# Row maxima of an attention encoder from the queries' high halves, four key blocks of a query tile in one go

## The chip, the cores and the metric

The kernel runs on one core of one Trainium2 chip. The metric is the device time of one execution in microseconds, as the median of several runs; smaller is better. PE is the matrix engine, DVE the vector engine, ACT the scalar engine, POOL the general-purpose engine, SP the engine that issues most DMAs. PSUM is the memory into which PE writes; DVE and ACT read it.

## The reference

Two layers, each on 2048 positions of 1024 features. A layer normalises, projects to seven column groups, mixes one half by a gated spatial product within chunks of 128 positions, and runs attention on the other half: 8 query heads, 2 key/value heads of 64 channels, query and key normalised and rotated, every query against all 2048 keys.

```python
sc = jnp.einsum('bqkgd,bskd->bkgqs', qblk, k).astype(jnp.float32) * scale
p = jax.nn.softmax(sc, axis=-1).astype(v.dtype)
return jnp.einsum('bkgqs,bskd->bqkgd', p, v)
```

The concatenated halves, each multiplied by a gate, go through an output projection, a second normalisation and the residual sum. Softmax gives the same result whatever number is subtracted from a whole row of scores, as long as nothing overflows; the kernel subtracts an approximate row maximum.

## The kernel before

All float32 operands of the large products are split into two float16 halves, high and low, and each product is made of three float16 products. Queries lie in DRAM as `q_d[group][head]`, two halves of 64 channels each by 512 positions; keys lie in SBUF as `k_st`, where the key's high half stands twice, in rows 0 to 63 and again in rows 64 to 127, and as `k_lo`, its low half with two rows of ones.

A layer has two stages. In the first the projections run, 24 matmuls to an accumulation (`pp`), and a list of background jobs with due times (`bg`) is stepped along with them; each step gives out up to two jobs that are due. In the second stage attention runs over units: a unit is one of 4 groups of 512 queries (`qb`) with one of 8 heads, 32 units a layer. A unit goes over 16 key blocks of 128 keys; an iteration `k` of the main loop is one key block, 512 in a layer. In an iteration PE makes the scores (`sp`, keys by 512 queries, two matmuls: `k_st` with both query halves stacked in 128 rows, and `k_lo` with the query's high half and the maxima in 66 rows). ACT takes the exponential twice, to float16 (`p_parts`) and to float32 (`p_f`); POOL, and DVE in 15 of 100 iterations, subtract the one from the other for the low half; three iterations later PE multiplies both halves with the values (`po`, 12 matmuls). Jobs for certain iterations stand in a table `later` (written by `at`), and a list `fill` is spread over the iterations; it holds the output projection of the group before (`pout`). It begins 16 iterations after a group's last unit.

The shift of the scores must be known before a unit's attention begins. So the row maxima are made ahead, with queries in the output's rows: for each of a unit's 4 query tiles of 128 queries (`j`) and each of 4 key blocks of 512 keys (`c`), PE makes one matmul `pmax` of the tile's queries, high and low half stacked in 128 rows, against `k_st`, and DVE reduces it to a column of `mx` (`max_step`; 16 steps to a unit, 1024 in all). `max_row` takes the maximum over the 4 columns, `stack_max` transposes it (`t<-ident,m_neg`) and stores it as two float16 rows. The first 8 units of a layer are done as background jobs at the end of the projection stage (the calls in `before`, L860 on DVE), one step per job. The other 24 are placed in the attention iterations, 16 steps of a unit spread over 20 iterations, so that four iterations in five have one.

Every PSUM tile, `sp`, `pmax`, `pp`, `pout`, `po`, `py` and the transposes alike, comes from one pool of 8 buffers, each a whole bank. A buffer given out again waits for the last reader of what it held. PE, DVE, ACT and POOL work off their instructions strictly in the written order; in the attention stage all of it is pinned (the class `Pinned`, whose helper is line 87, so most instructions there carry L87).

Of the kernel before, what the change touches and what calls it, by code (L numbers as in the profile page):

```python
# [14 lines left out]
ALU = mybir.AluOpType  # L15
AX = mybir.AxisListType
# [3 lines left out]
P = 128  # L20
D = 1024
ND = D // P
GRP = 512
TPG = GRP // P
NH = 8
HD = 64
# [16 lines left out]
def encoder(ctx: ExitStack, tc, x, w_in, w_out, pre_g, post_g, ln_a_g, ln_a_b,  # L43
            spatial_w, spatial_b, q_norm_g, k_norm_g, rope, out):
    nc = tc.nc
# [3 lines left out]
    NG = S // GRP  # L49
# [18 lines left out]
    def f_t(name, n=GRP, dt=F32):  # L68
        return fp.tile([P, n], dt, name=name, tag="f")
# [4 lines left out]
    def ps_t(name):  # L74
        return psum.tile([P, GRP], F32, name=name, tag="ps", bufs=8)
# [14 lines left out]
    PE, ACT, DVE, POOL = Pinned(nc.tensor), Pinned(nc.scalar), Pinned(nc.vector), Pinned(nc.gpsimd)  # L90
# [9 lines left out]
    q_d = [dram.tile([NH, 2, HD, GRP], F16, name=f"q_d{g}") for g in range(NG)]  # L100
# [86 lines left out]
    bg = Background()  # L187
# [616 lines left out]
    def attend(l, kv, nxt):  # L804

        k_st, k_lo, _, v16 = kv
# [25 lines left out]
        def at(k, f):  # L832
            later.setdefault(k, []).append(f)

        state = [Obj() for _ in units]
        pairs = [Obj() for _ in range(len(units) // 2)]

        def load_qm(u):
            qb, h = units[u]
            s = state[u]  # L840
            s.qm = f_t("q_m", dt=F16)
            nc.sync.dma_start(s.qm, q_d[qb][h].rearrange("a d t -> (a d) t"))
            s.mx = small.tile([P, TPG, NG], F32, name="mx", bufs=3)

        def load_q(u):
            qb, h = units[u]
            s = state[u]
            s.qs = f_t("q_st", dt=F16)
            nc.sync.dma_start(s.qs, q_d[qb][h].rearrange("a d t -> (a d) t"))
            s.q2 = f_t("q2", dt=F16)  # L850
            nc.sync.dma_start(s.q2[0:HD], q_d[qb][h, 0])
            nc.sync.dma_start(s.q2[HD:HD + 2], m_d[qb][h])

        def max_step(u, n, pe, dve):
            s = state[u]
            j, c = n // NG, n % NG
            kv = units[u][1] // (NH // NKV)
            ps = ps_t("pmax")
            pe.matmul(ps, s.qm[:, j * P:(j + 1) * P], k_st[:, kv, c * GRP:(c + 1) * GRP], start=True, stop=True)
            dve.tensor_reduce(s.mx[:, j, c:c + 1], ps, AX.X, ALU.max)  # L860

        def max_row(u, dve):
            s = state[u]
            s.m = small.tile([P, TPG], F32, name="m_neg", bufs=3)
            dve.tensor_reduce(s.m, s.mx, AX.X, ALU.max, negate=True)

        def stack_max(u, pe, act, dve):
            s = state[u]
            qb, h = units[u]
            ps = ps_t("t2")  # L870
            pe.transpose(ps[0:TPG, 0:P], s.m, ident)
            for i in range(2):
                rows = small.tile([TPG, P], F16, name="m_rows", bufs=4)
                if i == 0:
                    hi = rows
                    act.activation(rows, ps[0:TPG, 0:P], AF.Copy, bias=EXP_SHIFT)
                else:
                    dve.scalar_tensor_tensor(rows, ps[0:TPG, 0:P], EXP_SHIFT, hi, ALU.add, ALU.subtract)
                nc.sync.dma_start(m_d[qb][h, i].rearrange("(t p) -> t p", p=P), rows)
# [327 lines left out]
        steps = TPG * NG  # L1207
        span = ((len(units) - 1) * NT - 16) // (len(units) - pre)

        def before():  # L1210

            n0 = 0
            for u in range(pre):
                bg.add(max(n0 - 10, 0), lambda u=u: load_qm(u))
                for n in range(steps):
                    bg.add(n0 + 4 + n, lambda u=u, n=n: max_step(u, n, PE, nc.vector))
                bg.add(n0 + steps + 6, lambda u=u: max_row(u, nc.vector))
                bg.add(n0 + steps + 8, lambda u=u: stack_max(u, PE, nc.scalar, nc.vector))
                n0 += steps
            bg.add(n0 + 4, lambda: load_q(0))  # L1220
            bg.add(n0 + 4, lambda: load_qm(pre))

        def first_wo():
# [4 lines left out]
            for f in wout_steps(range(4), nc.scalar, nc.vector):  # L1228
                f()

        yield before, first_wo
        both = [w_t([P, 8, GRP], "p_parts", F16) for _ in range(2)]
        both = [b[:, n] for b in both for n in range(8)]
# [18 lines left out]
        for u in range(pre, len(units)):  # L1252
            k0 = (u - pre) * span
            if k0 >= 8:
                at(k0 - 8, lambda u=u: load_qm(u))
            for n in range(steps):
                at(k0 + n * span // steps, lambda u=u, n=n: max_step(u, n, PE, DVE))
            at(k0 + span + 1, lambda u=u: max_row(u, DVE))
            at(k0 + span + 5, lambda u=u: stack_max(u, PE, ACT, DVE))

# [51 lines left out]
        for k in range(end + 4):  # L1312
            if k < total:
                u, i = k // NT, k % NT
                s = state[u]
                kv = units[u][1] // (NH // NKV)
# [23 lines left out]
            if 0 <= kb < total:  # L1340
                u, i = kb // NT, kb % NT
                s = state[u]
                kv = units[u][1] // (NH // NKV)
# [16 lines left out]
        n = 0  # L1360
# [27 lines left out]
    for l in range(DEPTH):  # L1388
        k_t = big_t([P, 2, NKV, S], "k_t", F16)
        kv = [k_t[:, 0], k_t[:, 1]]  # L1390
        v_t = big_t([P, 2, NT * NKV * HD], "v_st")
        kv.append(v_t.bitcast(F32)[:, 0].rearrange("p (t k d) -> p t k d", t=NT, k=NKV))
        v_h = v_t.bitcast(F16).rearrange("p a n -> p (a n)")[:, 4 * NT * NKV * HD - NT * NKV * VW:]
        kv.append(v_h.rearrange("p (t k d) -> p t k d", t=NT, k=NKV))
        att = attend(l, kv, layers[l + 1] if l + 1 < DEPTH else None)
        layers[l].run(kv, layers[l].first, *next(att))
        for _ in att:
            pass
# [40 lines left out]
```

## Time and profile before

| what | us |
|---|---|
| median of three runs | 2554.7 |
| lowest and highest run | 2548.59, 2555.02 |
| the profiled execution's own time | 2549.72 |
| its span from first to last instruction | 2547.9 |
| PE busy in it | 2461.1 |
| DVE, ACT, POOL busy | 1833.9, 1558.3, 1151.0 |
| attention stage of layer 1, about | 593 to 1259 |
| attention stage of layer 2, about | 1854 to 2512 |

In a row of the page's groups stand the source line, engine, operation, what is written and read, the tile's size, the count, the busy time and the mean duration of one in ns, then the idle time before them and who ended it. PE's durations are modelled and overlap, so the spacing of starts is what a matmul costs. ACT's and DVE's records overlap a little too. In a row of the timeline stand the start in us, the time from the start of the first to the end of the last instruction merged in it, and the count; in brackets, the idle time before it and who ended it.

### The profile page before, as it was taken

The numbers are of one execution on the slowest core, as the hardware profiler recorded it, in microseconds if no ns is written. First come the engines' busy times: TensorE is split into PE (matmuls) and PEld (weight loads), VectorE is DVE, ScalarE is ACT, GpSimd is POOL, SyncE is SP. The second block draws the span as 40 slices with busy tenths as digits, with TensorE's granted clock in tenths as the row PEclk, the third lists the DMA queues.
The fourth block names the chain that finished last, engine by engine and source line by source line (L and its number), as shares of the span: only waits on it lengthen the run. The fifth ranks groups of instructions, "written<-read, shape, count | busy, mean of one in ns | idle before, by whom it ended". The sixth has DMA issues, their size and how long they took to land. (4 is left out here: it accounts for less than half of the span.)

```text
span 2547.9 us, 61817 instructions
## 1 busy us (share of the span) xinstructions
PE 2461.1 (97%) x24938; PEld 1634.4 (64%) x24938; DVE 1833.9 (72%) x4138; ACT 1558.3 (61%) x3219; POOL 1151.0 (45%) x968
## 2 busy tenths in 40 slices
PE   6999999999999999999989999999999999999997
PEld 5888876445665666665569887754456666656653
DVE  6676677886767787778377666778777767776765
ACT  6643212116998888898645522111289988888884
POOL 0000110005888777787530011100078877777875
PEclk9999999999999999999989999999999999999999
DMA  5254212211221221221433622122222212221213
GB/s 189 88 170 126 59 37 87 67 55 60 78 72 57 74 78 52 84 88 60 158 125 100 194 76 67 50 80 56 67 68 66 74 53 74 62 67 52 70 53 129
DMA packets 224963, 211.64 MB, mean 83 GB/s; under 512 B 44834, under 2 KB 194978, under 8 KB 224676
## 3 DMA queue, kind: packets, MB, share of 16 engines
q1 hardware_dynamic: 224676, 207.69, 26.5%
q8 instruction: 195, 3.19, 0.5%
q14 instruction: 92, 0.75, 0.1%
HBM read 140.92 MB, written 66.72 MB: 81 GB/s over the span
## 5 line engine op out<-in xcount | busy, mean ns | idle before, releaser
L87 POOL TENSOR_TENSOR p_parts<-p_f,p_parts 128x512 f16<-128x512 f32 x872 | 1040.3, 1208 | 568.1 <-ACT p_f L87 514.6
L87 ACT ACTIVATE p_parts<-sp 128x512 f16<-128x512 f32 x1024 | 629.8, 615 | 160.3 <-PE sp L87 125.9
L87 PEld LDWEIGHTS <-p_parts 128*128 128x128 f16 x12288 | 511.7, 97 | 257.5 <-DVE p_parts L87 7.4
L87 PE MATMUL pp<-w_hl,hT 128*128 128x256 f16 x5376 | 637.8, 275 | 8.3 <-ACT w_hl L324 4.7
L87 ACT ACTIVATE p_f<-sp 128x512 f32<-128x512 f32 x1024 | 629.9, 615 | 0.0
L87 DVE TENSOR_REDUCE mx<-pmax 128x1 f32<-128x512 f32 x768 | 512.9, 680 | 120.8 <-PE pmax L87 119.1
L87 PEld LDWEIGHTS <-hT 128*128 128x128 f16 x5376 | 520.6, 99 | 83.7 <-issue 13.0
L87 PE MATMUL po<-v_st,p_parts 128*128 128x65 f16 (+1 forms) x12288 | 545.6, 193 | 11.5 <-DVE p_parts L87 6.4
L87 PE MATMUL pout<-wo,y_t 128*128 128x512 f16 x1488 | 462.7, 379 | 0.2
L87 PE MATMUL pmax<-k_t,q_m 128*128 128x512 f16 x1024 | 389.2, 381 | 8.7 <-DVE mx L860 7.7
L87 PE MATMUL sp<-q,k_t 66*128 66x512 f16 x1024 | 390.8, 382 | 0.0
L87 PE MATMUL sp<-q_st,k_t 128*128 128x512 f16 x1024 | 388.4, 379 | 1.9 <-DVE mx L87 0.9
L87 PE MATMUL pp<-hT,w_hl 128*128 128x512 f16 x1536 | 380.7, 383 | 0.0
L87 PEld LDWEIGHTS <-w_hl 128*128 128x128 f16 x1536 | 148.3, 99 | 181.7 <-issue 15.0
L87 PEld LDWEIGHTS <-y_t 128*128 128x128 f16 x1488 | 144.8, 98 | 170.0 <-issue 3.5
L860 DVE TENSOR_REDUCE mx<-pmax 128x1 f32<-128x512 f32 x256 | 169.2, 681 | 28.9 <-PE pmax L87 28.4
L87 PEld LDWEIGHTS <-q_m 128*128 128x128 f16 x1024 | 101.1, 99 | 119.7 <-issue 1.4
L427 POOL TENSOR_TENSOR fa<-fa,gain_q 128x512 f32<-128x512 f32 x16 | 21.6, 1352 | 325.1 <-DMA fa<-in_rope_dram 175.0
L524 POOL TENSOR_TENSOR fl<-fv,fh 128x512 fp32r<-128x512 f32 x32 | 42.6, 1351 | 251.3 <-ACT fh L523 224.7
L87 DVE TENSOR_TENSOR p_parts<-p_f,p_parts 128x512 f16<-128x512 f32 x152 | 119.6, 787 | 38.8 <-ACT p_f L87 38.4
L555 ACT ACTIVATE pp<-fa 128x512 f32<-128x512 f32 x32 | 19.3, 602 | 188.8 <-DVE fa L554 188.8
L87 PEld LDWEIGHTS <-k_t 128*128 128x128 f16 (+1 forms) x2048 | 131.5, 98 | 4.7 <-issue 1.4
(206 smaller groups left out, 2194.0 us busy)
## 6 DMA issues: line engine op xcount, KB each, us to landing
w_raw<-in_w_in_dram SPq DMA_DIRECT2D x13, 1024.0 KB
x_t<-in_x_dram SPq DMA_DIRECT2D x16, 512.0 KB
gb_d<-fa SPq DMA_DIRECT2D x32, 256.0 KB
w_raw<-in_w_in_dram SPq DMA_DIRECT2D x16, 512.0 KB
wo_row<-in_w_out_dram SPq DMA_DIRECT2D x16, 512.0 KB
wo_raw<-in_w_out_dram SPq DMA_DIRECT2D x16, 512.0 KB
z_d<-fb SPq DMA_DIRECT2D x32, 256.0 KB
fb<-z_d SPq DMA_DIRECT2D x32, 256.0 KB
```

The lines of the kernel that those rows point to most:

```text
L87: return tc.keep_in_program_order(call(*args, **kw))
L427: nc.gpsimd.tensor_tensor(cs, cs, gain.unsqueeze(1).broadcast_to([P, TPG, 2, HD]), ALU.mult)
L524: nc.gpsimd.tensor_tensor(s.lo, vh, s.hi.bitcast(F32), ALU.subtract)
L555: nc.scalar.activation(pg, th, AF.Square, accum_out=self.ysq[:, g, c:c + 1])
L860: dve.tensor_reduce(s.mx[:, j, c:c + 1], ps, AX.X, ALU.max)
```

## The change

The tile of queries `q_m` holds the high half twice, in rows 0 to 63 and 64 to 127, loaded by two DMAs, in place of the high and the low half by one. The maxima are therefore those of the high half's scores. `max_tile` gives out the four matmuls of a query tile together, each over 64 rows: key blocks 0 and 2 use rows 0 to 63 of the queries and of `k_st`, key blocks 1 and 3 rows 64 to 127. Each has a PSUM buffer of its own, four at once. `max_reduce` is the reduction of one. In the projection stage a job is now a whole query tile with its four reductions; in attention a unit's four query tiles stand 5 iterations apart, two of the reductions in the same iteration and two in the next.

```diff
-            nc.sync.dma_start(s.qm, q_d[qb][h].rearrange("a d t -> (a d) t"))
+            for i in range(2):
+                nc.sync.dma_start(s.qm[i * HD:(i + 1) * HD], q_d[qb][h, 0])
...
-        def max_step(u, n, pe, dve):
+        def max_tile(u, j, pe):
+
             s = state[u]
-            j, c = n // NG, n % NG
             kv = units[u][1] // (NH // NKV)
-            ps = ps_t("pmax")
-            pe.matmul(ps, s.qm[:, j * P:(j + 1) * P], k_st[:, kv, c * GRP:(c + 1) * GRP], start=True, stop=True)
-            dve.tensor_reduce(s.mx[:, j, c:c + 1], ps, AX.X, ALU.max)
+            s.pm = [ps_t("pmax") for _ in range(NG)]
+            for c in range(NG):
+                r = slice(c % 2 * HD, c % 2 * HD + HD)
+                pe.matmul(s.pm[c], s.qm[r, j * P:(j + 1) * P], k_st[r, kv, c * GRP:(c + 1) * GRP],
+                          start=True, stop=True)
+
+        def max_reduce(u, j, c, dve):
+            s = state[u]
+            dve.tensor_reduce(s.mx[:, j, c:c + 1], s.pm[c], AX.X, ALU.max)
...
-                for n in range(steps):
-                    bg.add(n0 + 4 + n, lambda u=u, n=n: max_step(u, n, PE, nc.vector))
+                for j in range(TPG):
+                    def f(u=u, j=j):
+                        max_tile(u, j, PE)
+                        for c in range(NG):
+                            max_reduce(u, j, c, nc.vector)
+                    bg.add(n0 + 4 + NG * j, f)
...
-            for n in range(steps):
-                at(k0 + n * span // steps, lambda u=u, n=n: max_step(u, n, PE, DVE))
+            for j in range(TPG):
+                k1 = k0 + j * span // TPG
+                at(k1, lambda u=u, j=j: max_tile(u, j, PE))
+                for c in range(NG):
+                    at(k1 + c // 2, lambda u=u, j=j, c=c: max_reduce(u, j, c, DVE))
```

Two places show how instructions moved. The first is PE in the attention stage of layer 1, at the start of one iteration. Before:

```order
L87 MATMUL sp<-q_st,k_t 128x512
L87 LDWEIGHTS k_t
L87 MATMUL sp<-q_11543,k_t 128x512
L87 LDWEIGHTS q_m
L87 MATMUL pmax<-k_t,q_m 128x512
L87 LDWEIGHTS y_t
L87 MATMUL pout<-wo,y_t 128x512
```

And in the changed kernel, in an iteration that has maxima:

```order
L87 MATMUL sp<-q_11565,k_t 128x512
L87 LDWEIGHTS q_m
L87 MATMUL pmax<-k_t,q_m 128x512
L87 LDWEIGHTS q_m
L87 MATMUL pmax<-k_t,q_m 128x512
L87 LDWEIGHTS q_m
L87 MATMUL pmax<-k_t,q_m 128x512
L87 LDWEIGHTS q_m
L87 MATMUL pmax<-k_t,q_m 128x512
L87 LDWEIGHTS y_t
L87 MATMUL pout<-wo,y_t 128x512
```

One pmax in four iterations of five has become four in one iteration of five, each still with its weight load, between a score matmul and the output projection.

The second is DVE in the attention stage. Before, around the end of a unit:

```order
L87 TENSOR_TENSOR p_parts<-p_f,p_parts 128x512
L87 TENSOR_REDUCE mx<-pmax 128x1
L87 TENSOR_SCALAR rden<-po,cols 128x4
L87 RECIPROCAL rden<-rden 128x4
L87 TENSOR_TENSOR gb<-gb,rden 128x4x64
L87 TENSOR_SCALAR x_r<-o_t,rs_o 128x512
L87 TENSOR_REDUCE mx<-pmax 128x1
L87 TENSOR_TENSOR o_pair<-po,gb 128x4x64
```

And in the changed kernel:

```order
L87 TENSOR_TENSOR p_parts<-p_f,p_parts 128x512
L87 SCALAR_TENSOR_TENSOR o_t<-o_t,rs_o,x_r 128x512 x2
L87 TENSOR_REDUCE mx<-pmax 128x1 x2
L87 SCALAR_TENSOR_TENSOR y_t<-y_t,cols 128x4x128
L87 TENSOR_REDUCE mx<-pmax 128x1 x2
L87 TENSOR_SCALAR rs_m<-ss_o 128x1
```

The reductions come in two pairs, one iteration apart, with other work of that iteration between them.

## The prediction

> **What bounds the kernel now.** I read the page's busy times first, then the stretches, then the order of time around a score block, and last the pmax tile's waits.
>
> ```profile
> PE 2461.1 (97%) x24938; PEld 1634.4 (64%) x24938; DVE 1833.9 (72%) x4138; ACT 1558.3 (61%) x3219; POOL 1151.0 (45%) x968
> PEclk9999999999999999999989999999999999999999
> 421.00:592.00 171.00, 166.31 (x818) 80.63 (x817) 136.31 (x269) 32.36 (x72) 1.27 (x1) 0.98 0.19 56
> 745.60:780.80 35.20, 34.44 (x480) 21.96 (x477) 27.51 (x44) 33.27 (x68) 33.44 (x28) 1.00 0.26 62
> 780.80:1225.00 444.20, 440.94 (x5447) 268.65 (x5445) 340.80 (x686) 384.72 (x785) 336.64 (x278) 1.00 0.22 69
> L87 PE MATMUL pmax<-k_t,q_m 128*128 128x512 f16 x1024 | 389.2, 381 | 8.7 <-DVE mx L860 7.7 <-DVE hT L87 0.4 <-DVE mx L87 0.3
> ```
>
> In the stretch rows the columns after the length are PE, weight loads, DVE, ACT, POOL, clock, DMA share. PE is busy almost throughout at nearly full clock; nobody else is. The 381 ns of one pmax is a modelled duration that overlaps its neighbours, so a matmul's price has to be read from starts:
>
> ```profile
> 762.59 0.38 PE L87 MATMUL pmax<-k_t,q_m 128*128 128x512 f16 x1
> 762.81 0.53 PE L87 MATMUL po<-v_st,p_parts 128*128 128x65 f16 x12
> 763.17 0.38 PE L87 MATMUL sp<-q_st,k_t 128*128 128x512 f16 x1
> 763.39 0.38 PE L87 MATMUL sp<-q,k_t 66*128 66x512 f16 x1
> 763.61 0.38 PE L87 MATMUL pmax<-k_t,q_m 128*128 128x512 f16 x1
> 763.83 0.60 PE L87 MATMUL po<-v_st,p_parts 128*128 128x65 f16 x12
> 764.27 0.38 PE L87 MATMUL sp<-q_st,k_t 128*128 128x512 f16 x1
> ```
>
> From 763.61 to 763.83 a pmax takes 0.22 us of PE's time; 1024 of them take 0.22 ms of a span of 2.55 ms. The twelve po matmuls, each with its own weight load, take 0.36 us (762.81 to 763.17), so a float16 load and a short matmul together need 0.03. In the next block the same po take 0.44: they wait for POOL. This is a block without output-projection work, in the second stretch above, where POOL is busy 33.44 of 35.2 us; in the third, long stretch POOL has 24% to spare and ACT 13%, and PE decides.
>
> **The change, part by part.** *The pairs.* 256 bursts of four pmax replace 1024 single ones. A burst costs 4 x 0.22 = 0.87 us now (0.218 each before rounding). If two matmuls in the two row halves run side by side, the four take two streams, 0.44, and 0.03 for the second of the first pair, which starts one load later: 0.46. No trace row shows such a pair; the bounds are 0.46 (full overlap) and 0.87 (none). I take 0.46, because operands, array rows and PSUM banks of the two have nothing in common. The Trainium skill ("TensorE: Matmul & The Clock Gate", Part 3) says the same: matmuls in different row groups start about 4 ns apart, and four of them at K=32 gained 3.07 times. By its 4 ns the pair would cost 0.44, the burst 0.02 less; no run here shows it yet.
>
> *Entering and leaving the halves.* Before and after a burst stand matmuls over all 128 rows. The nearest rows are the one-row matmuls, which also use part of the array's rows, against the same size over all rows:
>
> ```profile
> 145.93 0.49 PE L87 MATMUL pp<-w_hl,hT 128*128 128x256 f16 x3
> 146.35 0.38 PE L87 MATMUL pt<-v_row,ones 1*128 1x1 f32 x2
> 146.66 0.28 PE L87 MATMUL pp<-w_hl,hT 128*128 128x256 f16 x1
> 1503.33 0.49 PE L87 MATMUL pp<-w_hl,hT 128*128 128x256 f16 x3
> 1503.66 0.28 PE L87 MATMUL pe<-w_col,ones 128*128 128x1 f32 x2
> 1503.80 0.27 PE L87 MATMUL pp<-w_hl,hT 128*128 128x256 f16 x1
> 146.35 0.29 PEld L87 LDWEIGHTS pt<-v_row,ones 1*128 1x128 f32 x2 [0.21 <-issue]
> 161.22 0.60 PE L87 MATMUL pt<-wsT,fb 128*128 128x256 f32 x2
> 161.75 0.69 PE L87 MATMUL pt<-sb_row,ones 1*128 1x256 f32 x2
> 162.38 0.72 PE L87 MATMUL pp<-w_hl,hT 128*128 128x256 f16 x5
> L87 PEld LDWEIGHTS pt<-ws,fh 128*128 128x128 f32 x256 | 41.2, 192 | 13.0 <-issue 4.9 <-DVE fc L443 3.0
> ```
>
> The full-row pair (pe) follows its three pp at once (1503.33 + 3 x 0.11 = 1503.66) and lasts 0.14. The one-row pair starts 0.09 late (145.93 + 0.33 = 146.26, start 146.35) with its weights not loaded ahead (its load starts with it), and the next pp comes 0.31 later: the visit costs 0.09 + 0.31 - 0.14 = 0.26. The second site: four float32 matmuls of 256 columns in 1.16 us (161.22 to 162.38) against 4 x 0.22 = 0.87: 0.29. In both, about 0.09 is a float32 weight load that isn't hidden, 192 ns against about 99 for float16:
>
> ```profile
> L87 PEld LDWEIGHTS <-q_m 128*128 128x128 f16 x1024 | 101.1, 99 | 119.7 <-issue 1.4 <-DVE o_pair L87 0.8
> ```
>
> A visit with float16 weights is therefore 0.17 to 0.20; I take 0.20, with 0.29 as the dear end. Nothing is the cheap end: the transposed maxima, which use only 4 of the array's columns, cost no gap:
>
> ```profile
> 762.26 0.38 PE L87 MATMUL sp<-q,k_t 66*128 66x512 f16 x1
> 762.48 0.27 PE L87 MATMUL t<-ident,m_neg 128*4 128x128 f32 x1
> ```
>
> They start 0.22 after the sp before them, and the pmax follows 0.11 later. The Trainium skill ("TensorEngine Tiling (Array Packing)", Key Properties) has the rule that changing the tiling mode drains TensorE, and it speaks against this change. The one-row visits agree, with 0.09 lost on entry; the four-column ones show no drain. By the rule each burst pays twice, by the four-column row not at all: the sum below would be 51 us better.
>
> So a burst costs 0.46 + 0.20 = 0.66 instead of 0.87: 0.21 saved, **54 us** over 256 bursts, 13 in the projections' tails (64 bursts) and 41 in the attention stages (192).
>
> *Four banks at once.* PSUM's 8 buffers of one tag are shared by everything, and a burst now takes four in a row. The matmul that needs the buffer next waits for an exponential or a reduction much nearer to it than before.
>
> ```profile
> 842.99 0.38 PE L87 MATMUL sp<-q_st,k_t 128*128 128x512 f16 x1
> 842.89 0.59 ACT L87 ACTIVATE p_f<-sp 128x512 f32<-128x512 f32 x1
> 843.63 0.60 ACT L87 ACTIVATE p_parts<-sp 128x512 f16<-128x512 f32 x1
> 844.12 0.59 ACT L87 ACTIVATE p_f<-sp 128x512 f32<-128x512 f32 x1
> 764.46 0.28 DVE L87 SCALAR_TENSOR_TENSOR m_rows<-t,m_rows 4x128 f16<-4x128 f32 x1 [2.66 <-ACT m_rows L87]
> 764.66 1.27 DVE L87 TENSOR_REDUCE mx<-pmax 128x1 f32<-128x512 f32 x2
> ```
>
> An sp buffer is free 1.72 us after its matmul starts (842.99 to 844.12 + 0.59). A pmax buffer is free after 1.0 us at best (0.38 for the matmul's record, 0.6 for one of the two reductions) and after 2.3 us here (763.61 to 764.66 + 1.27, DVE having sat waiting for ACT). In the written order some matmuls now stand nearer than that behind the one whose result must first be read: counted with the matmul prices above, 1.72 us for ACT and 1.8 for DVE (between the two ends), about 50 waits of the attention stages come due too early, 18 us together (4 of them, 0.1 us, in the old order); with 2.3 us for DVE 91 waits and 40 us. They aren't independent, one late start gives the next more room. I take 18, bounds 0 and 45. Behind a late sp or pmax stands all of PE's queue.
>
> *The projections' tails.* DVE is fuller there (136.31 of 171 us), and PE already stops for it once, then runs at half rate:
>
> ```profile
>   DVE mx L860: 7.7, 4
> 428.30 1.66 DVE L325 SCALAR_TENSOR_TENSOR w_hl<-w_raw,w_col,w_hl 128x256 f16<-128x256 f32 x4
> 430.62 0.59 PE L87 MATMUL pmax<-k_t,q_m 128*128 128x512 f16 x1 [3.66 <-DVE mx L860]
> 430.99 1.92 PE L87 MATMUL pp<-hT,w_hl 128*128 128x512 f16 x4
> 432.70 0.63 PE L87 MATMUL pmax<-k_t,q_m 128*128 128x512 f16 x1
> ```
>
> After the 3.66 us wait four pp take 1.71 us (430.99 to 432.70), 0.43 each, twice the usual. A burst's four reductions need 4 x 0.6 = 2.4 us of DVE in one go, and the burst after it stands only about 4.1 us later (16 pp at 0.216 and 0.66). I charge one more such stop per layer, 3.7 + 0.4, 8 us together: 5 of the 13 stay.
>
> *Blocks without output-projection work,* 16 of each query tile's 128, go at POOL's pace (rows above); an eighth of the 41, **5 us**, isn't got.
>
> *Edits at nothing.* The query load is two DMAs of 64 rows in place of one of 128: 64 more issues on SP.
>
> ```profile
> L842 SPq DMA_DIRECT2D q_m<-q_d x64: 319/383/1595, 416.1 to 2397.1; - x64
> ```
>
> At 0.38 us each that is 25 us of a queue that mostly waits; the load is given out 8 key blocks (some 9 us) before use. Uncovered, it would cost 0.38 per unit. The reductions stay 1024 in number on DVE, two in the burst's block and two in the next; max_row comes no later than it did. Using the high half alone shifts the maximum slightly and alters no count.
>
> **Sum.** 54 - 18 - 8 - 5 = 23 us off the profiled execution's 2549.7 gives 2527. The median of the runs shown, 2554.7, lies 5 above that execution, so I expect **2532** for the median (0.9% faster).
>
> **Rivals.**
> *The pairs don't overlap* (slower). Place: every burst. If the second of a pair streams only after the first, a burst costs 0.87 + 0.20 = 1.07, 0.20 more than now: +51, with the 8 of DVE's stops about +59: 2614. It decides from the point where the second of a pair starts more than 0.12 us after the first (0.03 is charged, and the 23 us left are 0.09 for each of 256 bursts). For it: nothing in this trace has ever run side by side on PE. Against: weight loads and matmuls already overlap, and the halves share no operand.
> *The banks take it all.* Same pairs, but waits of 40 in attention and a stop more in the tails: 54 - 40 - 12 - 5 is 3 us lost: 2558. For it: DVE's 2.66 us wait above, and half rate after a stop. Against: PE lost only 0.3 to L87's mx before.
> *The halves are free to enter.* Like the four-column transposes: 51 more, 74 off in all: 2480.
> *The change doesn't do what it says* only as in the first rival: the order shows the four matmuls together everywhere.
>
> **How the numbers follow.** Forecast 0.58 (its own range 2500 to 2548: waits of 0 to 35), no overlap 0.14, banks 0.20 (2540 to 2568), free entry 0.08. The range 2490 to 2605 leaves out most of the last and half of the first rival, and nothing between. A measurement of this kernel can tell about 0.3%, 8 us, from no change. Faster: 0.53 of the forecast, 0.08 of free entry, 0.05 of banks, 0.66. Same: 0.04 and 0.10, 0.14. Slower: 0.14, 0.05 and 0.01, 0.20.
>
> **What the new profile would show.** Right: the two pmax of a pair starting within 0.05 us, the third 0.22 after the first; the burst's first about 0.1 after its turn; the matmul after it 0.1 later than a stream; 0.66 from a burst's first pmax's turn to the next matmul. PE's idle before pmax, 8.7 us now, and before sp rising to about 30 together with ACT's p_f and DVE's mx as releasers. POOL's share up, the first stretch of each query tile unchanged. Wrong: pmax 0.22 apart in a burst; a burst over 0.87; PE waiting more than 50 us; a clock below 0.97.

## The result

The changed kernel takes 2568.7 us (median of four runs, 2567.07 to 2570.47) against 2552.3 for the kernel before beside it (2548.59 to 2555.02). The ratio is 1.0066, with an interval of 1.0048 to 1.0083: slower by 0.66%, 16 us, where the prediction said faster by 0.9%. The profiled execution took 2569.01 us, its span 2567.2: 19.3 us more than the 2547.9 of before. These 19.3 are what has to be explained.

The page of the changed kernel, its busy times and two of its groups:

```profile
PE 2439.6 (95%) x24938; PEld 1553.4 (61%) x24938; DVE 1829.0 (71%) x4138; ACT 1552.7 (60%) x3219; POOL 1155.6 (45%) x968
L87 PE MATMUL pmax<-k_t,q_m 64*128 64x512 f16 x1024 | 176.9, 383 | 31.0 <-DVE mx L867 16.6
L87 PE MATMUL po<-v_st,p_parts 128*128 128x65 f16 (+1 forms) x12288 | 547.5, 193 | 16.9 <-DVE p_parts L87 11.0
```

PE is busy 21.5 us less and the span is 19.3 us longer. The idle time before pmax went from 8.7 to 31.0 us, and DVE's reductions end most of it. Idle is counted here only beyond the modelled end of the matmul ahead, 0.38 us after its start, though the next one could have started 0.22 after it; so this row tells less than what was lost.

The view by stretches (length, then busy time of PE, weight loads, DVE, ACT, POOL, then clock and DMA), cut at each layer's first pmax, first sp and last unit. Before:

```profile
420.30:590.40 170.10, 165.41 (x814) 80.19 (x813) 135.64 (x273) 32.59 (x72) 1.27 (x1) 0.98 0.19 56
590.40:1261.30 670.90, 662.33 (x8342) 405.94 (x8341) 494.18 (x948) 590.45 (x1193) 522.01 (x436) 1.00 0.24 74
1682.50:1851.30 168.80, 164.06 (x814) 79.71 (x813) 135.38 (x273) 32.60 (x72) 1.27 (x1) 0.99 0.19 56
1851.30:2514.00 662.70, 656.90 (x8308) 401.19 (x8307) 456.50 (x830) 576.89 (x1145) 518.32 (x436) 1.00 0.23 70
```

And the changed kernel:

```profile
422.40:594.40 172.00, 162.94 (x813) 70.23 (x813) 132.97 (x271) 32.32 (x72) 1.27 (x1) 0.96 0.20 56
594.40:1277.30 682.90, 656.02 (x8341) 376.23 (x8340) 496.79 (x948) 589.04 (x1193) 524.25 (x436) 1.00 0.24 73
1696.70:1868.20 171.50, 162.33 (x813) 70.00 (x813) 133.17 (x273) 32.32 (x72) 1.27 (x1) 0.96 0.19 56
1868.20:2533.20 665.00, 648.07 (x8309) 371.04 (x8307) 453.66 (x830) 573.73 (x1145) 520.52 (x436) 1.00 0.23 70
```

The projections' tails lost 1.9 and 2.7 us, the attention stages 12.0 and 2.3. The clock (1.00 is full) is full in attention in both, so it has no part in the loss there. In the tails it fell from 0.98 and 0.99 to 0.96.

**The pairs do run side by side.** One undisturbed burst of the changed kernel in the timeline, matmuls and weight loads:

```profile
1040.95 0.38 PE L87 MATMUL sp<-q_st,k_t 128*128 128x512 f16 x1
1041.17 0.38 PE L87 MATMUL sp<-q,k_t 66*128 66x512 f16 x1
1041.48 0.12 PEld L87 LDWEIGHTS <-q_m 64*128 64x128 f16 x4 [0.42 <-issue]
1041.48 0.61 PE L87 MATMUL pmax<-k_t,q_m 64*128 64x512 f16 x4
1042.02 0.11 PEld L87 LDWEIGHTS <-y_t 128*128 128x128 f16 x2 [0.42 <-issue]
1042.02 0.39 PE L87 MATMUL pout<-wo,y_t 128*128 128x512 f16 x1
```

Four pmax lie within 0.61 us from the first start to the last end, which leaves two streams: the four starts are 0, 3, 226 and 229 ns. The next matmul comes 0.54 us after the first. The Trainium skill ("TensorE: Matmul & The Clock Gate", Part 3) gives about 4 ns between matmuls of different row groups; the trace agrees, with 3 ns. Ahead of the burst stand 0.31 us instead of 0.22: its weight load starts together with its first matmul, not ahead of it. The same happens to pout's load behind the burst. An undisturbed burst thus costs 0.54, the 0.09 ahead of it and 0.01 on the matmul behind it, 0.64 us, where four single pmax cost 0.87: 0.23 saved, 59 us over 256 bursts. 193 of the 256 have this pattern (135 of 192 in attention, 58 of 64 in the tails).

**Waits for PSUM buffers take it back.** In a tail of the changed kernel (PE and DVE rows of the timeline; brackets hold the idle time and who ended it):

```profile
478.46 0.69 DVE L867 TENSOR_REDUCE mx<-pmax 128x1 f32<-128x512 f32 x1
478.76 0.81 PE L87 MATMUL pmax<-k_t,q_m 64*128 64x512 f16 x3
479.06 1.67 DVE L325 SCALAR_TENSOR_TENSOR w_hl<-w_raw,w_col,w_hl 128x256 f16<-128x256 f32 x4
480.64 0.68 DVE L867 TENSOR_REDUCE mx<-pmax 128x1 f32<-128x512 f32 x1
481.38 0.37 PE L87 MATMUL pmax<-k_t,q_m 64*128 64x512 f16 x1 [1.81 <-DVE mx L867]
```

The fourth pmax takes a buffer that the reduction of 480.64 has to give back. That reduction stands behind four w_hl instructions on DVE, and PE starts 0.06 us after it ends. In attention:

```profile
725.56 0.38 PE L87 MATMUL sp<-q_st,k_t 128*128 128x512 f16 x1
726.19 0.60 ACT L87 ACTIVATE p_parts<-sp 128x512 f16<-128x512 f32 x1 [0.37 <-PE sp L87]
726.20 0.60 PE L87 MATMUL pmax<-k_t,q_m 64*128 64x512 f16 x3
726.69 0.59 ACT L87 ACTIVATE p_f<-sp 128x512 f32<-128x512 f32 x1
727.33 0.37 PE L87 MATMUL pmax<-k_t,q_m 64*128 64x512 f16 x1 [0.53 <-ACT p_f L87]
```

The fourth pmax takes the buffer of the scores made just ahead of the burst, and starts 0.05 us after ACT's second exponential is through with them. At that moment all eight buffers are held: `po` and `pout`, which collect over many key blocks, `py` and `t`, which wait to be read, the scores, and the burst's first three. The fourth should have followed the third within 3 ns and came 0.90 later: more than this burst could ever save.

I counted such starts over the whole trace: a PE instruction that starts right behind the end of the last reader of the buffer it takes, with its delay over the usual spacing. Before, they cost 13 us (tails 9.0, attention 2.5 and 1.4); in the changed kernel 71 us (24.2, 27.8 and 19.2), 58 more. By reader, of the 47 in attention: ACT's p_f 23 in 65 waits, DVE's mx 8 in 28, and 16 in 37 for the readers of pout, py and pt (mostly DVE's o_t, y_lo and hT). In the tails 22 of the 24 are DVE's mx.

This count lacks one reader, DVE's o_pair, which gives back the buffer of po. The view of waits of the changed kernel has it (idle us in total, times, longest):

```profile
PE pmax L87 <- DVE o_pair L87: 3.8, 6, 1.6
PE sp L87 <- DVE o_pair L87: 1.7, 3, 0.7
```

By the same rule, starts behind an o_pair cost 12 us in 18 waits of the changed kernel and 1 in 4 of the kernel before, about 10 more.

Two smaller losses come on top. Behind the stop in the tail, shown above, the granted clock falls. In the columns of the stretch rows, the first row is the sixteen pp that follow it, at a clock of 0.67, and the second the sixteen behind the next burst:

```profile
481.69:486.93 5.24, 5.24 (x17) 1.87 (x17) 3.82 (x7) 0.00 (x0) 0.00 (x0) 0.67 0.33 78
487.47:491.03 3.56, 3.56 (x18) 1.48 (x17) 3.56 (x7) 0.00 (x0) 0.00 (x0) 1.00 0.48 142
```

Added up over both tails, the slow spacing of pp costs 10 us in the changed kernel and 3.5 before, some 6 more. And po waits 5 us more: 16.9 us of idle time in its row above, against 11.5 before:

```profile
L87 PE MATMUL po<-v_st,p_parts 128*128 128x65 f16 (+1 forms) x12288 | 545.6, 193 | 11.5 <-DVE p_parts L87 6.4
```

With 59 saved and 58, 10, 6 and 5 lost, the sum is 20 us, for the 19.3 to be explained. The terms are good to some 5 us each: a second count of the buffer waits, with the lower quartile of each pair of instructions' spacings as the usual one, gives 66 where the first has 71, and 13 again for the kernel before. The 64 transposed maxima add no term of their own. A pmax starts 0.205 us behind one where a burst follows, and 0.11 before the change, but these 0.09 are the burst's entry, which its 0.64 holds already.

### The profile page after: what moved, and what is told of

It reads as the page before. It is cut to its first block, busy times and chain, and to the rows that moved or that the text cites. A ratio compares the mean times of both kernels' runs of the same rounds, so it can differ in the third digit from the quotient of the medians.

```text
span 2567.2 us, 61924 instructions
## 1 busy us (share of the span) xinstructions
PE 2439.6 (95%) x24938; PEld 1553.4 (61%) x24938; DVE 1829.0 (71%) x4138; ACT 1552.7 (60%) x3219; POOL 1155.6 (45%) x968
## 5 line engine op out<-in xcount | busy, mean ns | idle before, releaser
L87 PE MATMUL po<-v_st,p_parts 128*128 128x65 f16 (+1 forms) x12288 | 547.5, 193 | 16.9 <-DVE p_parts L87 11.0
L87 DVE TENSOR_REDUCE mx<-pmax 128x1 f32<-128x512 f32 x768 | 482.9, 677 | 38.5 <-PE pmax L87 38.5
L87 PE MATMUL pp<-hT,w_hl 128*128 128x512 f16 x1536 | 362.2, 389 | 0.5 <-DVE mx L867 0.5
L87 PEld LDWEIGHTS <-y_t 128*128 128x128 f16 x1488 | 139.5, 99 | 223.5 <-issue 82.4
L87 PE MATMUL pmax<-k_t,q_m 64*128 64x512 f16 x1024 | 176.9, 383 | 31.0 <-DVE mx L867 16.6
L867 DVE TENSOR_REDUCE mx<-pmax 128x1 f32<-128x512 f32 x256 | 160.2, 681 | 22.9 <-PE pmax L87 22.9
L555 ACT ACTIVATE pp<-fa 128x512 f32<-128x512 f32 x32 | 19.2, 601 | 218.6 <-DVE fa L554 218.6
L536 DVE SCALAR_TENSOR_TENSOR fb<-pt,lng,zbias 64x128 f32<-64x128 f32 x256 | 89.3, 349 | 36.2 <-PE pt L87 32.0
```

The lines of the kernel that those rows point to most:

```text
L87: return tc.keep_in_program_order(call(*args, **kw))
L536: nc.vector.scalar_tensor_tensor(s.zt[r, c, :], pz[r, h * P:(h + 1) * P], self.lng[r, c:c + 1], self.zbias[r, c, :], ALU.mult, ALU.add)
L555: nc.scalar.activation(pg, th, AF.Square, accum_out=self.ysq[:, g, c:c + 1])
L867: dve.tensor_reduce(s.mx[:, j, c:c + 1], s.pm[c], AX.X, ALU.max)
```

## The experiments

Each was timed beside the kernel before on the same chip; that one took between 2550.8 and 2552.8 us. "Waits for buffers" means the first count above, without o_pair.

**Bursts without row halves.** The four pmax of a tile are given out together as in the change, but each over 128 rows, high and low half of the queries stacked.

```diff
...
-                r = slice(c % 2 * HD, c % 2 * HD + HD)
-                pe.matmul(s.pm[c], s.qm[r, j * P:(j + 1) * P], k_st[r, kv, c * GRP:(c + 1) * GRP],
+                pe.matmul(s.pm[c], s.qm[:, j * P:(j + 1) * P], k_st[:, kv, c * GRP:(c + 1) * GRP],
```

> The four matmuls of a query tile stay together, but each uses all 128 rows and both query halves again, so there are no pairs and no entering or leaving of row halves; a burst's matmuls cost PE 0.87 us, as single ones did. Theory 'banks' (four PSUM buffers claimed in a row make PE wait for ACT's and DVE's readers): the time lies over the kernel before by the waits, 25 to 60 us, 2575 to 2610, with sp, pmax and pout released by p_f and mx in the trace. Rival 'halves' (what eats the gain is the switching of the array or another cost of the row halves): no switch here, so 2552, as before, within 5 us.

Measured: 2591.8 us, ratio 1.015 (1.013 to 1.0171). PE's work is that of the kernel before, no half is entered, and it is 40 us slower. Waits for buffers are 44 us, 31 more than before. Giving the four out together costs by itself; the halves win back 23 us of it, not 59.

**Pairs two at a time.** The row halves stay, but two pmax are given out every two or three key blocks, with two buffers; the tails get pairs in the same way (left out here).

```diff
...
-            for j in range(TPG):
-                k1 = k0 + j * span // TPG
-                at(k1, lambda u=u, j=j: max_tile(u, j, PE))
-                for c in range(NG):
-                    at(k1 + c // 2, lambda u=u, j=j, c=c: max_reduce(u, j, c, DVE))
+            for n in range(2 * TPG):
+                k1 = k0 + n * span // (2 * TPG)
+                cs = (n % 2 * 2, n % 2 * 2 + 1)
+                at(k1, lambda u=u, j=n // 2, cs=cs: max_tile(u, j, cs, PE))
+                for c in cs:
+                    at(k1, lambda u=u, j=n // 2, c=c: max_reduce(u, j, c, DVE))
```

> The same pairs in row halves, but given out two at a time, 2.5 iterations apart, both reductions in the same iteration; 512 visits to the halves instead of 256, two PSUM buffers claimed at once instead of four. A pair costs PE 0.003 + 0.305 + 0.093 = 0.40 us by the bursts' starts in the changed kernel, against 0.436 for two single ones: 18 us saved, 6 of them lost where the transposed maxima now stand before a pair. Theory 'banks': waits shrink to about 10 us over those of before, 2545 to 2555, faster than the changed kernel. Rival 'halves': twice the visits, so the 75 us between the ideal and the measured time of the changed kernel double, 2600 to 2640.

Measured: 2564.0 us, ratio 1.004 (1.0027 to 1.0054), outside both expected ranges. One pair in its timeline:

```profile
801.13 0.38 PE L87 MATMUL sp<-q,k_t 66*128 66x512 f16 x1
801.44 0.39 PE L87 MATMUL pmax<-k_t,q_m 64*128 64x512 f16 x2
801.76 0.60 PE L87 MATMUL pout<-wo,y_t 128*128 128x512 f16 x2
```

0.31 before it and 0.32 behind its first pmax: with the 0.01 that the matmul behind it loses, a pair costs 0.42 against 0.436 for two single pmax. 512 visits eat the overlap. Waits for buffers are only 22 us, so fewer buffers do remove most of the waits; but a visit has to be shared by more than two pmax to gain, and that takes the buffers.

**One PSUM buffer less**, in both kernels, one line each:

```diff
-        return psum.tile([P, GRP], F32, name=name, tag="ps", bufs=8)
+        return psum.tile([P, GRP], F32, name=name, tag="ps", bufs=7)
```

The changed kernel:

> The changed kernel with 7 PSUM buffers instead of 8, nothing else. Theory 'banks': it is on the steep part, one buffer less costs 25 to 80 us, 2595 to 2650. Rival 'halves', and rival 'pacing' (iterations of uneven length, 1.0 and 1.7 us, run ACT and POOL idle and then late): the buffers aren't what is waited for, within 8 us of 2569.

The kernel before:

> The kernel before with 7 PSUM buffers instead of 8. All theories: single maxima leave buffers to spare, 0 to 10 us over 2552. If it loses as much as the changed kernel does with 7, the pool was short already and the burst isn't special.

Measured: the changed kernel 2661.7 us, ratio 1.0428 (1.04 to 1.0455), 93 us over the same kernel with 8; the kernel before 2576.1, ratio 1.0091 (1.0068 to 1.0114), 24 us over its own time. What pmax waited for, changed kernel with 7 buffers (us, times):

```profile
  ACT p_f L87: 32.1, 58
  DVE mx L867: 16.4, 12
  DVE o_pair L87: 6.9, 9
  DVE o_t L87: 5.6, 8
```

and with 8:

```profile
  DVE mx L867: 16.6, 8
  ACT p_f L87: 5.4, 10
  DVE o_pair L87: 3.8, 6
```

Both lost more than expected (25 to 80 and 0 to 10), so the kernel before wasn't free of such waits either; but a buffer is worth four times as much to the changed kernel. The count of waits rises from 71 to 170 us there and from 13 to 34 in the kernel before, by nearly what the times rise (99 for 93, 21 for 24). That is the check on the count: it follows the time when nothing but the buffers is changed. With the second count and o_pair's waits the rises are 92 and 24.

**The reductions at once.** All four in the burst's own key block, in place of two and two.

```diff
-                    at(k1 + c // 2, lambda u=u, j=j, c=c: max_reduce(u, j, c, DVE))
+                    at(k1, lambda u=u, j=j, c=c: max_reduce(u, j, c, DVE))
```

> The changed kernel with all four reductions of a burst on DVE in the burst's own iteration, instead of two there and two in the next. Theory 'banks', the readers on DVE being late: the third and fourth buffer come free up to an iteration earlier, 2555 to 2565. If the waits that count are those for ACT's exponentials: 2566 to 2572, as the changed kernel (2569).

Measured: 2569.7 us, ratio 1.0067 (1.0052 to 1.0082), no different from the change, as expected if the waits that count are those for ACT's exponentials. Waits for buffers stay at 71 us: DVE's mx falls from 8.0 to 6.3 us in attention, the other readers rise from 15.8 to 17.5.

**The burst at the end of its key block**, behind pout and po instead of right behind the scores, with the reductions one block later.

```diff
...
-                at(k1, lambda u=u, j=j: max_tile(u, j, PE))
+                at(k1, lambda u=u, j=j: max_tile(u, j, PE), after_po)
                 for c in range(NG):
-                    at(k1 + c // 2, lambda u=u, j=j, c=c: max_reduce(u, j, c, DVE))
+                    at(k1 + 1 + c // 2, lambda u=u, j=j, c=c: max_reduce(u, j, c, DVE))
...
+            for f in after_po.pop(k, []):
+                f()
```

> The changed kernel with the burst at the end of its iteration, behind the output projection and the po matmuls, about 0.8 us later for ACT to have read the scores; the reductions one iteration later too. Theory 'banks', the readers on ACT being late: the burst's own waits for p_f (15 us in the changed kernel's attention stages) go, 2552 to 2562. If DVE's reductions are what is late, or uneven iterations: 2566 to 2572.

Measured: 2564.3 us, ratio 1.0054 (1.0035 to 1.0074), 4 us under the change, within its interval and between the two expected ranges. Waits for buffers are 78 us, not fewer. The burst's own waits for p_f do go (pmax sits idle for them 0.5 us, 5.4 in the changed kernel), but the next scores take them over (sp 10.9 us, 3.1 before the move). What is won is in po's waits for the low halves, 6.7 us of idle time where 14.3 stood.

**The change in attention alone.** The tails keep single pmax over 128 rows, as before; their units load the low half again.

```diff
-                nc.sync.dma_start(s.qm[i * HD:(i + 1) * HD], q_d[qb][h, 0])
+                nc.sync.dma_start(s.qm[i * HD:(i + 1) * HD], q_d[qb][h, i if u < pre else 0])
...
-                for j in range(TPG):
-                    def f(u=u, j=j):
-                        max_tile(u, j, PE)
-                        for c in range(NG):
-                            max_reduce(u, j, c, nc.vector)
-                    bg.add(n0 + 4 + NG * j, f)
+                for n in range(steps):
+                    bg.add(n0 + 4 + n, lambda u=u, n=n: max_step(u, n, PE, nc.vector))
```

> Bursts in the attention stages alone; the 8 units at the end of each projection stage have single maxima over all rows with both query halves, as before the change. By the stages' lengths in the two traces the tails lost 1.9 and 2.7 us: 2564 if the tails are independent of the rest. If the clean price of a burst (0.23 us saved) had been realised in the tails, their 64 bursts would be missed: 2584.

Measured: 2567.7 us, ratio 1.0058 (1.0043 to 1.0073). The tails are back at 169.0 and 170.2 us (172.0 and 171.5 in the changed kernel) and their waits at 8.8, but the kernel gains 1 us only, less than the interval. In the tails as in attention the bursts' saving and their waits are of one size.

**POOL takes all the subtractions**, so that DVE has 152 instructions less in attention.

```diff
-    SHARE_0 = 15
-    SHARE = 15
+    SHARE_0 = 0
+    SHARE = 0
```

> The changed kernel with all low halves of the exponentials subtracted on POOL, none on DVE (152 instructions of 0.8 us leave DVE). Theory 'banks' with DVE's queue as the cause of the late reductions: 2550 to 2562, if POOL, at 1.12 us for each block of 1.3, keeps up. If ACT's reading is what is late: 2569 or, by POOL, slower, up to 2600.

Measured: 2572.4 us, ratio 1.0074 (1.0058 to 1.009). The time doesn't fall. The waits counted fall from 71 to 67 us, but those behind DVE's o_pair rise (pmax sits idle for it 11.1 us in 10 waits, 3.8 in 6 with the change), so that together they don't fall either: what DVE does for the subtractions is not what makes most of them.

**A microsecond of PE's work.** In both kernels 2 of the 4 products of the low value half are left out in every key block, so the output lacks that small term for two query tiles of four. Ten po then take 0.30 us instead of twelve in 0.36: 61 us of PE's time in all.

```diff
-                    PE.matmul(s.av[:, j, 0:HD], lhs, v_lo, start=False, stop=False, skip_group_check=True)
+                    if j % 2 == 0:
+                        PE.matmul(s.av[:, j, 0:HD], lhs, v_lo, start=False, stop=False, skip_group_check=True)
```

The kernel before:

> The kernel before with 2 of the 4 products of the low value half left out in every key block (query tiles 1 and 3), so the output lacks that small term there: 2048 po matmuls of 0.03 us, 61 us of PE's work in the attention stages. If PE's own work sets the end of the kernel before there, most of it is won, less what the key blocks at POOL's pace (an eighth) keep: 45 to 58 us, 2494 to 2507. If other engines set it, under 30 us: over 2522.

The changed kernel:

> The changed kernel with the same 2048 po matmuls left out. If PE waits there for readers of PSUM (the buffers theory), a microsecond taken from PE's work is partly waited again, and less is won than in the kernel before: 20 to 40 us, 2529 to 2549. If the visits' price on PE is all that ate the gain (rival), as much is won as in the kernel before, 45 to 58 us: 2511 to 2524.

Measured: before 2511.2 us, ratio 0.9841 (0.9825 to 0.9858), 40 us won; changed 2537.9, ratio 0.9953 (0.9938 to 0.9968), 31 us under its own time. Of 61 us taken from PE two thirds arrive in the kernel before, less than I had expected, and half in the changed one, within the range expected. Waits for buffers rise from 13 to 17 us in the one and from 71 to 89 in the other: the faster PE runs into the same readers earlier. The two gains differ by 9 us, not much more than their intervals allow; the count shows it more clearly than the times.

**The two kindest places together**: single pmax in the tails, the burst behind po in attention, its four reductions in the next key block. The edits are those of the change in attention alone and of the burst at the end of its key block, but for one line:

```diff
-                    at(k1 + 1 + c // 2, lambda u=u, j=j, c=c: max_reduce(u, j, c, DVE))
+                    at(k1 + 1, lambda u=u, j=j, c=c: max_reduce(u, j, c, DVE))
```

> The two kindest places together: single steps over all 128 rows in the projections' tails as before (their queries' low half loaded again), and in attention the burst at the end of its iteration, behind pout and po, with its four reductions in the next iteration. The tails alone were worth 1 us, the burst's place 4 us, so 2563 to 2565 if both gains add. If the buffers theory is right no place makes the burst cheap and it stays above 2556; if place was the trouble it comes under 2552.

Measured: 2576.7 us, ratio 1.0106 (1.009 to 1.0122). It stays above 2556, as the buffers theory has it, but the two gains do not add: it is 8 us slower than the change. Waits for buffers are 60 us, as the two edits let expect; the loss is elsewhere. What po waited for, here (us, times):

```profile
  DVE p_parts L87: 13.1, 14
  POOL p_parts L87: 5.6, 10
```

and with the burst behind po but the reductions two and two:

```profile
  POOL p_parts L87: 5.9, 12
  DVE p_parts L87: 0.8, 2
```

Four reductions in one go, 0.68 us each, hold up DVE's share of the subtractions, and po waits 12 us more for it (in a profiled execution of 2583.2 us, the slowest of four). The same four did no such harm in the burst's own key block (the reductions at once, above); that they do here may be their place right ahead of a subtraction, which I did not separate.

**The visit by itself.** The kernel before, with each of its 1024 single pmax over rows 0 to 63 alone, at the same places and with one buffer each. The maxima are those of the high half.

```diff
-            pe.matmul(ps, s.qm[:, j * P:(j + 1) * P], k_st[:, kv, c * GRP:(c + 1) * GRP], start=True, stop=True)
+            pe.matmul(ps, s.qm[0:HD, j * P:(j + 1) * P], k_st[0:HD, kv, c * GRP:(c + 1) * GRP], start=True, stop=True)
```

> The kernel before with each of its 1024 single pmax taken over rows 0 to 63 alone (the queries' high half), at the same places in the order and with the same one PSUM buffer each: every one is now a visit to a row half without a partner, and nothing is given out together. It measures the visit's price by itself. By the changed kernel's trace a visit costs 0.093 to enter and about 0.10 to leave, 0.19 in all: 1024 visits cost 195 us, and where POOL sets the pace (an eighth of the attention's 768) 18 less, so 2720 to 2760. If visits were cheap, and only the buffers ate the changed kernel's gain (rival), under 2650.

Measured: 2738.8 us, ratio 1.0734 (1.0717 to 1.0752). 186 us for 1024 visits are 0.182 each, with waits for buffers at 9 us, below those of the kernel before, and po's idle time at 4.1 us where it was 11.5. In its timeline:

```profile
800.61 0.38 PE L87 MATMUL sp<-q,k_t 66*128 66x512 f16 x1
800.93 0.39 PE L87 MATMUL pmax<-k_t,q_m 64*128 64x512 f16 x1
801.25 0.54 PE L87 MATMUL po<-v_st,p_parts 128*128 128x65 f16 x12
```

0.32 on each side of the pmax where 0.22 stood: by the starts, with the 0.01 on the matmul behind it, going and coming back costs PE 0.20 us, of which 0.18 show in the time, because other waits shrink. The Trainium skill ("TensorEngine Tiling (Array Packing)", Key Properties) says that a change of tiling mode drains TensorE; the trace agrees in that time is lost at both changes.

## Why the prediction was wrong

The mechanism on PE was right and its size nearly exact. The mechanism of the buffers was named too, but its term was mis-sized, and it decides the sign.

- **The pair's overlap**, 0.46 us of stream in a burst: right. The second of a pair starts after 3 ns, the third after 226. The rival "the pairs don't overlap" is out.
- **The visit**, 0.20 us: right. 0.093 on entry, 0.09 on exit and 0.01 behind it in the trace; the visits measured alone give 0.20 by their starts and 0.182 in the time. The rival of free entry is out.
- **The burst**, 0.66 us and 54 us saved: 0.64 and 59. Right.
- **Banks in attention**, 18 us with bounds of 0 and 45: this step failed. It measured 53, outside its bounds: 43 by the first count (47 less the 4 of before) and 10 behind o_pair (48 in all by the second count). Two things were wrong in it. The delays stood for each engine by one figure. Over all 1024 sp of the trace before, a score's buffer comes free 1.72 us after its matmul at the least and in the median, but after 2.03 or more in a quarter and 2.28 or more in a tenth; a wait is made by the late ones. For pmax I charged 1.8 us; in the changed kernel, whose reductions come in bunches, the median over 1024 is 2.7 and a quarter take 3.6 or more (before: 1.55 and 2.4). So buffers of sp and pmax cost 31 us in 93 waits, not 18 in 50. And the count took in only buffers of sp and pmax, though a burst takes those of pout, po, py and pt too: their readers make the other 16 us, in 37 waits, and o_pair's 12 in 18. That one late start gives the next more room was my reason to stay low; the waits grow when PE is faster, and with 7 buffers they more than double, so they leave each other little.
- **The tails**, 8 us: 15 in waits and some 6 by the slower clock behind them, for which the prediction had charged little. The stop is the one foreseen (four reductions in one go behind DVE's w_hl), and there are more of them: 22 us behind DVE's mx in 12 waits, 9 in 6 before. The prediction's sign of a clock below 0.97 came true in the tails, with 0.96.
- **Blocks at POOL's pace**, 5 us not got: right that nothing is won there. Thirty such key blocks (124 to 153 of a layer) take 31.4 us before and 32.3 after. That po waits 5 us more in all matches the figure partly by luck: the rise stands at DVE's share of the low halves (6.4 to 11.0 us), while POOL's falls (4.3 to 3.3).
- **The transposed maxima**, taken as the cheap end of a visit: they show no gap among full-row matmuls, and a burst behind one pays the same entry of 0.093 as behind a score. They said nothing about the price of a half.
- **The two query loads**, nothing: no wait for them shows on PE in the changed kernel. Right.

By these sizes the sum is 59 - 53 - 21 - 5, 20 us lost, where the prediction had 23 us won; 35 of the 43 between them are the banks in attention. The rival "the banks take it all" named the cause, with 3 us lost, and was nearer with its 40 in attention and 12 in the tails, but short in both. The test that the prediction set itself, PE waiting more than 50 us, came out against it, with 71 by the first count alone.

Layer 1's attention lost 12 us and layer 2's 2. Of the 10 between them 7 are in the count of buffers (25 and 18 more than before) and the other 3 behind o_pair (7 and 4 us, 0.6 in each before). What stays open is why layer 1 waits more. DVE is fuller there (497 of 683 us against 454 of 665 in the stretch rows), but giving DVE's subtractions to POOL won nothing, so the cause was not shown.

## What to carry to other kernels

In this kernel row halves do double the rate of the small matmuls, but each visit costs about 0.2 us of a stream of full-row matmuls. Two that shared it gained next to nothing and four gained 0.23 us; and as many results as share it want buffers at the same time, of which others hold some for long. Before bunching, count for each buffer which reader gives it back and how late that reader can be, for every kind of tile and with the late tail of each delay, not its median. Where PE is busy 97% of the time, taking work from it gains only as far as the readers of PSUM keep up: here two thirds of it, and half once the matmuls were bunched.

## What the runs showed of the hardware

The price of a visit looks like a weight load that isn't hidden. In the views of waits, the changed kernel's loads

```profile
PEld L87 <- issue: 291.7, 649, 5.1
```

and those of the kernel before (us in total, times, longest):

```profile
PEld L87 <- issue: 35.7, 76, 4.6
```

The loads stand still for nothing visible 649 times instead of 76. At every change between all rows and a half, the load starts within some ns of its matmul, and lasts 92 to 97 ns, which is the delay of that matmul (93 ns on entry, 92 on exit). That the one is the cause of the other I infer from the equal lengths; no run separated them, and by the records the delay lies ahead of the load as well as of the matmul. Within a burst, the loads of the second pair start 11 ns behind the first pair's matmuls and are hidden, though they go to the same two halves. The Trainium skill ("TensorE: Matmul & The Clock Gate", Part 3) says, of what overlaps, that loads overlap matmuls in flight only where the row group differs; here the loads of the same half did. Its account of the mechanism allows one more case, a load into a background weight buffer, which no run here tells apart.
